# A two-layer encoder on one core: the second block's modulation is made in two pieces, x is loaded in three

## The chip, the cores and the metric

The kernel runs on one core of a Trainium2 chip. The metric is the device time of one execution in microseconds (us), the median of several runs. The engines of the core have short names: PE (TensorE, matrix products), DVE (VectorE), ACT (ScalarE), POOL (GpSimd), and SP (SyncE, which here issues the loads). Each engine works through a fixed list of instructions in order and waits on semaphores where an instruction needs another engine's result or a load.

## The reference

Two layers, a gated linear attention (GLA) and an S5 state-space layer, on one sequence of T = 256 frames with D = 2048 channels, all in float32. A vector c shifts and scales each layer's input. What is cut stands at the first part of layer 0, where the change lies:

```python
mod = jnp.einsum('bd,lde->lbe', jax.nn.silu(c), ada_w) + ada_b[:, None, :]
for i in range(DEPTH):
    shift, scale, gate = jnp.split(mod[i], 3, axis=-1)
    u = x * (1.0 + scale[:, None, :]) + shift[:, None, :]
...
    # GLA: u @ w_in, then
    q, k, v, z, g_lr = jnp.split(
        proj, [GLA_QK, 2 * GLA_QK, 2 * GLA_QK + D_INNER, 2 * GLA_QK + 2 * D_INNER], axis=-1)
```

So before v, q and k can be computed from any 128 channels of u, the shift and the scale of these channels are needed: each is a product of silu(c) (2048 long) with 128 columns of `ada_w`.

## The kernel before

**Tiles and blocks.** The 2048 channels are 16 k-tiles of 128 partitions. The projections v (4096 columns, 8 groups of 512) and q and k (2048 columns, 4 groups of 512, called q here) need all 16 k-tiles. The kernel runs through them in four blocks of k-tiles, `blocks` = (0,2), (2,4), (6,4), (10,6) (first k-tile, count), so that it can begin with the first two tiles of u while the modulation of the others is still being made. In a block, `vqk_steps` lists the steps: for each of the 8 groups of v, and then the 4 of q, one step for each pair of k-tiles (kp). A step loads 256 x 512 weights (`wload`, 0.5 MB), splits them into a high part (ACT, L145) and a low part (DVE, L146), and issues on PE 12 matmuls of 512 columns for v (`mv_step`, L167 to L169) or 24 of 256 for q (`st_step`, L180 to L182): high weights by high u, low weights by high u, high weights by low u. At the end of a block v's banks are copied to the buffer `vbig` by ACT (first block) or added to it by DVE (L357 before, L372 after the change); q's likewise (L371).

**u.** `u_make(k0, nk)` makes u for k-tiles in twos: PE transposes x (L334, tiles psx), DVE multiplies by the scale and adds the shift (L338, uf), ACT rounds to the high part (L321, u0h), DVE subtracts for the low part (L322, u0l). It runs at the start of each block, for that block's tiles.

**Modulation.** `ada_pe(l, part, k0, nk)` returns a list of operations that make nk k-tiles of the shift (part 0) or of the scale (part 1): nk loads of 1 MB from `ada_w` (tiles named a), each followed by 16/nk products, and at the end `mod_cols`. Without `dve` the products are PE matmuls into a bank psa (L265), copied to a row by ACT (L268). With `dve=True` DVE makes the row: a multiplication by one column of silu(c) (L257) and then a chain of 15 multiply-and-adds (L259), each of nk x 128 columns and each on the result of the last. `mod_cols` turns the row into columns by PE matmuls with one column (L236, psmod), and DVE adds the bias into `mods` (L239 for the shift, L241 for the scale).

**Order.** The main loop (L714 on) spreads the modulation operations for the next block, list `a` made from `pieces[n + 1]`, evenly among the steps of this block. In block 0 it also loads the last 1792 columns of x (after step 0), in block 1 small vectors. The loop's order goes to a scheduler that fixes each engine's list. All loads are issued by SP, in order; eight semaphores go round among them, so a load also waits for the landing of the eighth before. The weights' tiles "w" form a ring of 4 (with 2 more in this part), and a load into it waits until both the high and the low part of the tile last held there are done. x (tiles xrow), modulation tiles and u lie in other slots ("s8").

**Names.** In the lists, v020 is the bank for v group 0 of the block that begins with k-tile 2, frames 0; wv02, hiv02 and lov02 are the weights of v group 0 for kp 2 (k-tiles 4 and 5) and their high and low parts; row012, psa002 and psmod012 are of layer 0, part 1 or 0, k-tile 2 on. a0120 is the load number 0 for row012. Numbers behind an underscore tell tiles of one name apart.

Of the kernel before, what the change touches and what calls it, by code (L numbers as in the profile page):

```python
# [16 lines left out]
D = 2048  # L17
# [16 lines left out]
def trunk(ctx, tc, x, c, ln_g, ln_b, ada_w, ada_b, gla_w_in, gla_gate_w2, gla_gate_b, gla_norm_g,  # L34
# [3 lines left out]
    V, S, PE = nc.vector, nc.scalar, nc.tensor  # L38
# [187 lines left out]
    cz = tp.tile([P, 16, 32], F32, tag="cz", name="cz")  # L226
# [5 lines left out]
    def mod_cols(row, l, part, k0, nk):  # L232

        ps = psx(f"psmod{l}{part}{k0}")
        for i in range(nk):
            PE.matmul(ps[:, i:i + 1], lhsT=row[:, i * P:(i + 1) * P], rhs=ones[:, 0:1], start=True, stop=True)  # L236
        ab = abT[:, 32 * l + 16 * part + k0:32 * l + 16 * part + k0 + nk]
        if part == 0:
            V.tensor_tensor(mods[:, l, 0, k0:k0 + nk], ps[:, 0:nk], ab, op=ALU.add)  # L239
        else:  # L240
            V.scalar_tensor_tensor(mods[:, l, 1, k0:k0 + nk], ps[:, 0:nk], 1.0, ab, op0=ALU.add, op1=ALU.add)  # L241

    def ada_pe(l, part, k0, nk, dve=False):

        acc = [None]
        nr, wd = 16 // nk, nk * P

        def step(kq):
            w = s8t(f"a{l}{part}{k0}{kq}", [nr, wd])
            dma(w, ada_w[l, kq * nr * P:(kq + 1) * nr * P, part * D + k0 * P:part * D + k0 * P + wd].rearrange("(k p) c -> p k c", p=P))  # L250
            if dve:
                if kq == 0:
                    acc[0] = rp.tile([P, 512], F32, tag="row", name=f"row{l}{part}{k0}", bufs=2)
                for i in range(nr):
                    k, o = kq * nr + i, acc[0][:, :wd]
                    if k == 0:
                        V.tensor_scalar(o, w[:, i, :], cs[:, 0:1], None, op0=ALU.mult)  # L257
                    else:
                        V.scalar_tensor_tensor(o, w[:, i, :], cs[:, k:k + 1], o, op0=ALU.mult, op1=ALU.add)  # L259
                return  # L260
            if kq == 0:
                acc[0] = psx(f"psa{l}{part}{k0}")
            for i in range(nr):
                k, q = kq * nr + i, i % 4
                PE.matmul(acc[0][32 * q:32 * q + 32, :wd], lhsT=cz[:, k, :], rhs=w[:, i, :], start=(k < 4), stop=(k >= 12))  # L265
            if kq == nk - 1:
                row = rp.tile([P, 512], F32, tag="row", name=f"row{l}{part}{k0}", bufs=2)
                S.copy(row[:, :wd], acc[0][:, :wd])  # L268
                acc[0] = row

        return [lambda kq=kq: step(kq) for kq in range(nk)] + [lambda: mod_cols(acc[0], l, part, k0, nk)]

    gate_dst = [None, None]

# [37 lines left out]
    def x_load(c0, c1):  # L312
        if not xr:
            xr.extend([s8t(f"xrow{i}", [D]) for i in range(2)])
        for tt in range(2):
            dma(xr[tt][:, c0:c1], x[0, tt * P:(tt + 1) * P, c0:c1])
# [11 lines left out]
    def u_make(k0, nk):  # L328
        for k2 in range(k0, k0 + nk, 2):
            ps = psx(f"psx{k2}")  # L330
            for kk in range(2):
                for tt in range(2):
                    k = k2 + kk
                    PE.transpose(ps[:, kk * T + tt * P:kk * T + (tt + 1) * P], xr[tt][:, k * P:(k + 1) * P], ident)  # L334
            for kk in range(2):
                k = k2 + kk
                uf = tp.tile([P, T], F32, tag="uf", name=f"uf{k}", bufs=2)
                V.tensor_scalar(uf, ps[:, kk * T:(kk + 1) * T], mods[:, 0, 1, k:k + 1], mods[:, 0, 0, k:k + 1], op0=ALU.mult, op1=ALU.add)  # L338
                hilo(u0.hi(k), u0.lo(k), uf)
# [63 lines left out]
    S.copy(abT, ps[:, :64])  # L403

    blocks = ((0, 2), (2, 4), (6, 4), (10, 6))
    pieces = (((0, 2),), ((2, 4),), ((6, 4),), ((10, 4), (14, 2)))
    ada0[-1]()
    x_load(0, 256)
    early = more(2, 0)
# [302 lines left out]
        gl["ft"] = ft  # L712

    gate = gla_gate()  # L714
    for n, blk in enumerate(blocks):
        u_make(*blk)
        steps = vqk_steps(*blk)
        a = []
        if n + 1 < len(blocks):
            for pc in pieces[n + 1]:  # L720
                a += ada_pe(0, 0, *pc) + ada_pe(0, 1, *pc, dve=pc[0] < 10)
        done = 0
        for i, f_ in enumerate(steps):
            while done < len(a) * (i + 1) // len(steps):
                a[done]()
                done += 1
            f_()
            if n == 0 and i == 0:
                x_load(256, D)
            if n == 1 and i == 0:  # L730
                vectors()
            if n == 2:
                next(lam, None)
                if i == 8:
                    prep_small()
            elif n == 3:
                pump(V_RATE)
                if i >= GATE_AT:
                    next(gate, None)
        if n == 2:  # L740
            for _ in lam:
                pass
# [6 lines left out]
    for c0, w_, o in ((0, 4, 0), (1, 3, 4), (2, 2, 7)):  # L749
        a = s8t(f"qs{c0}", [8, w_, 64])  # L750
# [10 lines left out]
    for h in range(4):  # L761
        ps = psx(f"psst{h}")
        for cc, (r, a, b) in enumerate(((0, 0, 256), (64, 64, 256), (0, 256, 384), (64, 320, 384))):
            for t in range(2):
                PE.matmul(ps[r:r + 64, a:b], lhsT=kt[:, 2 * h + t, cc * 64:cc * 64 + 64], rhs=qs[cc][:, 2 * h + t, :],
                          start=(t == 0), stop=(t == 1))
# [593 lines left out]
```

## Time and profile before

| | us |
|---|---|
| three runs | 1855.99, 1858.26, 1859.24 |
| median | 1858.26 |
| profiled execution, whole | 1856.07 |
| its span | 1854.3 |
| mean granted clock of PE | 0.994 |

The span is the time from the first to the last instruction in the profiled execution; what lies around it is 1.8 us. The profiled execution is 2.2 us below the median. In the profile, a row of a timeline gives start, duration (summed where several like instructions follow each other, "x8"), engine, source line, operation, output and inputs, and in brackets the idle time before it with what ended it. The granted clock is 1.0 at full speed and 0.5 at half.

### The profile page before, as it was taken

What the parts mean: (1) busy time and instruction counts of PE and PEld (TensorE: products, weight loads), DVE (VectorE), ACT (ScalarE), POOL (GpSimd) and SP (SyncE); (2) the same over time, 40 slices, a digit from 0 to 9 for tenths busy, and PEclk for the clock granted to TensorE, in tenths of its full rate; (3) what the DMA queues carried; (4) which work ended last, traced back from release to release, by engine and by line L of the source; (5) the groups of instructions that cost most, each with busy time, mean ns of one, the idle gap of its engine ahead of it and who ended that gap; (6) DMA issues with size and microseconds to landing.
All of it is one profiled execution on the core that took longest, in us unless ns stands there. A gap on an engine that the chain in (4) does not pass through costs nothing.

```text
span 1854.3 us, 33845 instructions
## 1 busy us (share of the span) xinstructions
PE 1802.9 (97%) x13635; PEld 1587.3 (86%) x13635; DVE 1423.6 (77%) x1886; ACT 894.9 (48%) x1247; POOL 68.8 (4%) x76
## 2 busy tenths in 40 slices
PE   6999999999999999999999999999999999999997
PEld 3787798799999888799998999989888888888886
DVE  2788675989999988688799789888677775557556
ACT  3533365655556333654444444545544444444332
POOL 0000000000000000002222210000000000000000
PEclk9999999999999999999999999999999999999999
DMA  9887976789889998565555477899788886669653
GB/s 357 316 270 259 350 240 209 213 298 322 285 285 318 332 356 285 173 204 163 157 165 158 136 210 216 237 241 247 222 271 267 270 274 211 186 186 328 193 189 91
DMA packets 239494, 449.15 MB, mean 242 GB/s; under 512 B 19221, under 2 KB 45263, under 8 KB 238055
## 3 DMA queue, kind: packets, MB, share of 16 engines
q1 hardware_dynamic: 235400, 437.53, 73.5%
q0 software_dynamic: 3168, 8.41, 1.5%
q8 instruction: 107, 1.75, 0.4%
q10 hardware_dynamic: 768, 1.05, 0.2%
q14 instruction: 51, 0.41, 0.1%
HBM read 432.49 MB, written 14.42 MB: 241 GB/s over the span
## 4 chain that ended last, share of the span: by engine, by line
PE 70%; DVE 8%; DMA 4%; issue 2%; ACT 1%; SPq 0%; DVEq 0%; ACTq 0%
PE gl L192 13%; PE gl L193 6%; PE op L168 6%; PE op L169 6%; PE op L167 6%; PE z L182 3%; PE z L180 3%; PE z L181 3%; PE sz L180 3%; PE sz L182 2%; PE sz L181 2%; PE su L180 2%; PE su L181 2%; PE su L182 2%; DMA rb<-rec 1%
## 5 line engine op out<-in xcount | busy, mean ns | idle before, releaser
L146 DVE TENSOR_TENSOR logl<-wgl,higl 128x1024 fp32r<-128x1024 f32 x128 | 156.5, 1224 | 117.1 <-ACT higl L145 110.2
L145 ACT CAST higl<-wgl 128x1024 fp32r<-128x1024 f32 x128 | 134.3, 1050 | 174.6 <-PE gl L192 169.7
L192 PE MATMUL gl<-yp,higl 128*128 128x512 f32 x512 | 180.7, 398 | 0.1
L192 PE MATMUL gl<-yb,higl 128*128 128x512 f32 x512 | 178.7, 394 | 0.0
L145 ACT CAST hio<-wo 128x1024 fp32r<-128x1024 f32 x96 | 101.2, 1055 | 156.2 <-PE op L169 138.2
L146 DVE TENSOR_TENSOR loo<-wo,hio 128x1024 fp32r<-128x1024 f32 x96 | 117.3, 1223 | 67.0 <-ACT hio L145 66.4
L292 DVE SCALAR_TENSOR_TENSOR acc<-wa,cs,acc 128x512 f32<-128x512 f32 x215 | 160.8, 748 | 2.7
L180 PE MATMUL su<-u1h,hisu 128*128 128x256 f32 x512 | 151.8, 298 | 0.0
L180 PE MATMUL sz<-u1h,hisz 128*128 128x256 f32 x512 | 150.1, 293 | 1.2 <-ACT zs L1193 1.2
L180 PE MATMUL z<-u0h,hiz 128*128 128x256 f32 x512 | 148.7, 290 | 0.0
L181 PE MATMUL su<-u1l,hisu 128*128 128x256 f32 x512 | 146.0, 285 | 0.0
L182 PE MATMUL z<-u0h,loz 128*128 128x256 f32 x512 | 145.0, 283 | 0.9 <-DVE loz L146 0.9
L182 PE MATMUL sz<-u1h,losz 128*128 128x256 f32 x512 | 145.2, 284 | 0.4 <-DVE losz L146 0.4
L182 PE MATMUL su<-u1h,losu 128*128 128x256 f32 x512 | 145.5, 284 | 0.0
L181 PE MATMUL sz<-u1l,hisz 128*128 128x256 f32 x512 | 145.2, 284 | 0.0
L181 PE MATMUL z<-u0l,hiz 128*128 128x256 f32 x512 | 144.7, 283 | 0.0
L193 PE MATMUL gl<-yb,logl 128*128 128x256 f32 x512 | 142.7, 279 | 0.0
L193 PE MATMUL gl<-yp,logl 128*128 128x256 f32 x512 | 141.4, 279 | 0.0
L192 PEld LDWEIGHTS gl<-yp,higl 128*128 128x128 f32 x512 | 95.9, 188 | 23.7 <-issue 1.7
L145 ACT CAST hisz<-wsz 128x1024 fp32r<-128x1024 f32 x64 | 66.9, 1050 | 100.9 <-PE sz L181 66.2
L192 PEld LDWEIGHTS gl<-yb,higl 128*128 128x128 f32 x512 | 96.0, 187 | 22.4
L145 ACT CAST hisu<-wsu 128x1024 fp32r<-128x1024 f32 x64 | 66.8, 1049 | 92.8 <-PE su L181 79.7
(316 smaller groups left out, 5021.9 us busy)
## 6 DMA issues: line engine op xcount, KB each, us to landing
wgl<-in_s_w_glu SPq DMA_DIRECT2D x128, 512.0 KB, 4.6
wa<-in_ada_w SPq DMA_DIRECT2D x115, 512.0 KB, 4.9
a<-in_ada_w SPq DMA_DIRECT2D x32, 1024.0 KB, 10.9
wv<-in_gla_w_in SPq DMA_DIRECT2D x64, 512.0 KB, 6.1
wz<-in_gla_w_in SPq DMA_DIRECT2D x64, 512.0 KB, 5.2
wsu<-in_s_w_in SPq DMA_DIRECT2D x64, 512.0 KB, 3.8
wsz<-in_s_w_in SPq DMA_DIRECT2D x64, 512.0 KB, 4.1
wo<-in_s_w_out SPq DMA_DIRECT2D x64, 512.0 KB, 4.5
```

The costliest lines, as they stand in the source:

```text
L145: S.copy(hi, w)
L146: last_lo[0] = V.tensor_tensor(lo, w, hi.bitcast(F32), op=ALU.subtract).ins
L167: PE.matmul(banks[tt], lhsT=uh, rhs=hi[:, kk, :], start=(k == first), stop=False)
L168: PE.matmul(banks[tt], lhsT=uh, rhs=lo[:, kk, :], start=False, stop=False)
L169: PE.matmul(banks[tt], lhsT=ul, rhs=hi[:, kk, :], start=False, stop=(k == last))
L180: PE.matmul(o, lhsT=wh, rhs=u.hi(k), start=(k == first), stop=False)
L181: PE.matmul(o, lhsT=wh, rhs=u.lo(k), start=False, stop=False)
L182: PE.matmul(o, lhsT=wl, rhs=u.hi(k), start=False, stop=(k == last))
L192: PE.matmul(banks[f], lhsT=hi[:, kk, fs], rhs=u.both(k), start=(k == 0), stop=False)
L193: PE.matmul(banks[f][:, :T], lhsT=lo[:, kk, fs], rhs=u.hi(k), start=False, stop=(k == last))
L292: V.scalar_tensor_tensor(acc[0], w[:, kk, :], cs[:, k:k + 1], acc[0], op0=ALU.mult, op1=ALU.add)
```

## The change

The modulation of the second block, k-tiles 2 to 5, is made in two pieces of two k-tiles each instead of one of four. The scale of the first piece (DVE) comes first, then its shift (PE), then u for k-tiles 2 and 3; the same then for k-tiles 4 and 5. The last three operations for the second piece (the last PE products of the shift with the row's copy, its columns, and u for k-tiles 4 and 5) are kept back from block 0 and run in block 1, after its first two steps. These first steps are reordered, so that groups 0 and 1 of v use k-tiles 2 and 3 before either uses 4 and 5. For the later blocks, u is made in the block before, when the modulation is done. The PE products of these pieces are issued in twos (`pair`): two loads, then the products of both. x is loaded in columns 0 to 255, 256 to 767 (after step 1 of block 0) and 768 to 2047 (in block 1) instead of 0 to 255 and 256 to 2047. In the third piece of the list DVE still makes the scale, now ahead of the shift; for the last two pieces PE makes both, the scale in twos.

```diff
@@ -240,9 +240,10 @@
         else:
             V.scalar_tensor_tensor(mods[:, l, 1, k0:k0 + nk], ps[:, 0:nk], 1.0, ab, op0=ALU.add, op1=ALU.add)
 
-    def ada_pe(l, part, k0, nk, dve=False):
-
-        acc = [None]
+    def ada_pe(l, part, k0, nk, dve=False, pair=False):
+
+
+        acc, ws = [None], []
         nr, wd = 16 // nk, nk * P
 
         def step(kq):
@@ -258,17 +259,31 @@
                     else:
                         V.scalar_tensor_tensor(o, w[:, i, :], cs[:, k:k + 1], o, op0=ALU.mult, op1=ALU.add)
                 return
-            if kq == 0:
+            ws.append(w)
+            if not pair:
+                mults(kq)
+
+        def mults(kq):
+            if acc[0] is None:
                 acc[0] = psx(f"psa{l}{part}{k0}")
-            for i in range(nr):
-                k, q = kq * nr + i, i % 4
-                PE.matmul(acc[0][32 * q:32 * q + 32, :wd], lhsT=cz[:, k, :], rhs=w[:, i, :], start=(k < 4), stop=(k >= 12))
+            k = nr * (kq + 1 - len(ws))
+            while ws:
+                w = ws.pop(0)
+                for i in range(nr):
+                    q = k % 4
+                    PE.matmul(acc[0][32 * q:32 * q + 32, :wd], lhsT=cz[:, k, :], rhs=w[:, i, :], start=(k < 4), stop=(k >= 12))
+                    k += 1
             if kq == nk - 1:
                 row = rp.tile([P, 512], F32, tag="row", name=f"row{l}{part}{k0}", bufs=2)
                 S.copy(row[:, :wd], acc[0][:, :wd])
                 acc[0] = row
 
-        return [lambda kq=kq: step(kq) for kq in range(nk)] + [lambda: mod_cols(acc[0], l, part, k0, nk)]
+        ops = []
+        for kq in range(nk):
+            ops.append(lambda kq=kq: step(kq))
+            if pair and kq % 2:
+                ops.append(lambda kq=kq: mults(kq))
+        return ops + [lambda: mod_cols(acc[0], l, part, k0, nk)]
 
     gate_dst = [None, None]
 
@@ -403,7 +418,7 @@
     S.copy(abT, ps[:, :64])
 
     blocks = ((0, 2), (2, 4), (6, 4), (10, 6))
-    pieces = (((0, 2),), ((2, 4),), ((6, 4),), ((10, 4), (14, 2)))
+    pieces = (((0, 2),), ((2, 2), (4, 2)), ((6, 4),), ((10, 4), (14, 2)))
     ada0[-1]()
     x_load(0, 256)
     early = more(2, 0)
@@ -712,21 +727,32 @@
         gl["ft"] = ft
 
     gate = gla_gate()
+    u_make(*blocks[0])
     for n, blk in enumerate(blocks):
-        u_make(*blk)
         steps = vqk_steps(*blk)
         a = []
         if n + 1 < len(blocks):
             for pc in pieces[n + 1]:
-                a += ada_pe(0, 0, *pc) + ada_pe(0, 1, *pc, dve=pc[0] < 10)
+                dve = pc[0] < 10
+                a += ada_pe(0, int(dve), *pc, dve=dve) + ada_pe(0, int(not dve), *pc, pair=True)
+                a.append(lambda pc=pc: u_make(*pc))
+        over = []
+        if n == 0:
+
+            a, over = a[:-3], a[-3:]
+        elif n == 1:
+            steps[0:4] = [steps[0], steps[2], steps[1], steps[3]]
+            steps[1:2] = [lambda f_=steps[1]: (f_(), [g_() for g_ in late])]
         done = 0
         for i, f_ in enumerate(steps):
             while done < len(a) * (i + 1) // len(steps):
                 a[done]()
                 done += 1
             f_()
-            if n == 0 and i == 0:
-                x_load(256, D)
+            if n == 0 and i == 1:
+                x_load(256, 768)
+            if n == 1 and i == 3:
+                x_load(768, D)
             if n == 1 and i == 0:
                 vectors()
             if n == 2:
@@ -737,6 +763,7 @@
                 pump(V_RATE)
                 if i >= GATE_AT:
                     next(gate, None)
+        late = over
         if n == 2:
             for _ in lam:
                 pass
```

Products of a piece of two k-tiles have 256 columns instead of 512, and a load (1 MB in each case) carries 8 of them instead of 4.

The order of the engines' instructions moves at three places. The first is DVE's list in block 0, from the low half of the second v group on. Before:

```order
L146 TENSOR_TENSOR lov10_236<-wv10_233,hiv10_235 128x1024
L146 TENSOR_TENSOR lov20_264<-wv20_261,hiv20_263 128x1024
L146 TENSOR_TENSOR lov30_292<-wv30_289,hiv30_291 128x1024
L146 TENSOR_TENSOR lov40_322<-wv40_319,hiv40_321 128x1024
L239 TENSOR_TENSOR mods_108<-psmod002_339,abT_143 128x4
L146 TENSOR_TENSOR lov50_350<-wv50_347,hiv50_349 128x1024
L146 TENSOR_TENSOR lov60_372<-wv60_369,hiv60_371 128x1024
L257 TENSOR_SCALAR row012_391<-a0120_389,cs_101 128x512
```

With the change, the same place:

```order
L146 TENSOR_TENSOR lov10_248<-wv10_245,hiv10_247 128x1024
L146 TENSOR_TENSOR lov20_276<-wv20_273,hiv20_275 128x1024
L258 TENSOR_SCALAR row012_202<-a0120_200,cs_101 128x256
L260 SCALAR_TENSOR_TENSOR row012_202<-a0120_200,cs_101,row012_202 128x256 x7
L260 SCALAR_TENSOR_TENSOR row012_202<-a0121_233,cs_101,row012_202 128x256 x8
L241 SCALAR_TENSOR_TENSOR mods_108<-psmod012_267,abT_143 128x2
L146 TENSOR_TENSOR lov30_300<-wv30_297,hiv30_299 128x1024
L146 TENSOR_TENSOR lov40_324<-wv40_321,hiv40_323 128x1024
```

The whole row of the first piece's scale, sixteen operations, now stands between the low halves of v groups 2 and 3, with the addition that waits for PE's columns behind it; before, the row (of 512 columns) began after group 6. The second place is PE's list from the end of block 0 into block 1. Before:

```order
L182 MATMUL q303_559<-u0h0_109,loq30_563 128x256
L236 MATMUL psmod012_550<-ones0_84,row012_391 128x1 x4
L334 MATMUL psx2_594<-ident_89,xrow0_151 128x128
L334 MATMUL psx2_594<-ident_89,xrow1_152 128x128
L334 MATMUL psx2_594<-ident_89,xrow0_151 128x128
L334 MATMUL psx2_594<-ident_89,xrow1_152 128x128
L334 MATMUL psx4_607<-ident_89,xrow0_151 128x128
L334 MATMUL psx4_607<-ident_89,xrow1_152 128x128
L334 MATMUL psx4_607<-ident_89,xrow0_151 128x128
L334 MATMUL psx4_607<-ident_89,xrow1_152 128x128
L390 MATMUL psv_646<-ident_89,vr_640 128x104
```

With the change, block 0's last q matmul is followed at once by block 1's first steps (k-tiles 2 and 3), and the second piece's shift, columns and transposes stand behind these, ahead of the second pass of v group 0:

```order
L167 MATMUL v121_661<-hiv11_664,u0h0_109 128x512
L168 MATMUL v121_661<-lov11_665,u0h0_109 128x512
L169 MATMUL v121_661<-hiv11_664,u0l0_111 128x512
L274 MATMUL psa004_680<-a0040_582,cz_105 32x256 x8
L274 MATMUL psa004_680<-a0041_584,cz_105 32x256 x8
L236 MATMUL psmod004_699<-ones0_84,row004_697 128x1 x2
L349 MATMUL psx4_703<-ident_89,xrow0_151 128x128
L349 MATMUL psx4_703<-ident_89,xrow1_152 128x128
L349 MATMUL psx4_703<-ident_89,xrow0_151 128x128
L349 MATMUL psx4_703<-ident_89,xrow1_152 128x128
L167 MATMUL v020_624<-hiv02_718,u0h0_109 128x512
L167 MATMUL v021_625<-hiv02_718,u0h0_109 128x512
```

What stood at the boundary, four columns and eight transposes for four k-tiles, is now half in block 0 and half behind block 1's first two steps. The third place is DVE's list at block 1's beginning. Before, from the scale's addition on:

```order
L241 SCALAR_TENSOR_TENSOR mods_108<-psmod012_550,abT_143 128x4
L338 TENSOR_SCALAR uf2_599<-psx2_594,mods_108 128x256
L338 TENSOR_SCALAR uf3_603<-psx2_594,mods_108 128x256
L146 TENSOR_TENSOR lov02_652<-wv02_649,hiv02_651 128x1024
L322 TENSOR_TENSOR u0l0_111<-uf2_599,u0h0_109 128x256
L322 TENSOR_TENSOR u0l0_111<-uf3_603,u0h0_109 128x256
L338 TENSOR_SCALAR uf4_612<-psx4_607,mods_108 128x256
L338 TENSOR_SCALAR uf5_616<-psx4_607,mods_108 128x256
```

With the change, from the addition of the second piece's scale on:

```order
L241 SCALAR_TENSOR_TENSOR mods_108<-psmod014_540,abT_143 128x2
L258 TENSOR_SCALAR row016_655<-a0160_653,cs_101 128x512
L260 SCALAR_TENSOR_TENSOR row016_655<-a0160_653,cs_101,row016_655 128x512
L239 TENSOR_TENSOR mods_108<-psmod004_699,abT_143 128x2
L260 SCALAR_TENSOR_TENSOR row016_655<-a0160_653,cs_101,row016_655 128x512
L353 TENSOR_SCALAR uf4_708<-psx4_703,mods_108 128x256
L260 SCALAR_TENSOR_TENSOR row016_655<-a0160_653,cs_101,row016_655 128x512
L337 TENSOR_TENSOR u0l0_111<-uf4_708,u0h0_109 128x256
L353 TENSOR_SCALAR uf5_712<-psx4_703,mods_108 128x256
L146 TENSOR_TENSOR lov02_719<-wv02_716,hiv02_718 128x1024
L337 TENSOR_TENSOR u0l0_111<-uf5_712,u0h0_109 128x256
L260 SCALAR_TENSOR_TENSOR row016_655<-a0161_736,cs_101,row016_655 128x512 x2
```

The products of block 2's scale (row016) now begin here, among the second piece's u; thirteen of the row's sixteen operations stand between the shift's addition (L239) and the low half of v group 3 for kp 2 (lov32). Before, row016 began after the low half of v group 6.

## The prediction

> **What bounds the kernel now.** First the page: busy time, the 40 slices, the chain that ended last.
>
> ```profile
> span 1854.3 us, 33845 instructions
> PE 1802.9 (97%) x13635; PEld 1587.3 (86%) x13635; DVE 1423.6 (77%) x1886; ACT 894.9 (48%) x1247; POOL 68.8 (4%) x76
> PE   6999999999999999999999999999999999999997
> PE 70%; DVE 8%; DMA 4%; issue 2%; ACT 1%; SPq 0%; DVEq 0%; ACTq 0%
> ```
>
> PE is busy 97% of the span, so TensorE is the bound nearly everywhere, and an edit that leaves the number of matmuls alone can only win or lose the moments in which PE waits or runs at half clock. The change touches the order of work up to about 260 us; behind that every engine has the same instructions in the same order. So the time moves by as much as that place moves. Next, who PE waits for from 20 to 262 us (line, releaser, total, times, longest).
>
> ```profile
> PE v L168 <- DVE lov L146: 3.3, 5, 1.0
> PE psmod L236 <- DVE row L259: 2.8, 1, 2.8
> PE v L167 <- ACT u0h L321: 2.1, 2, 1.1
> PE v L167 <- ACT hiv L145: 1.9, 3, 0.6
> PE psa L265 <- DMA a<-in_ada_w: 1.1, 1, 1.1
> ```
>
> Some 11 us in all can be won here by perfect cover. The largest single wait, 2.8 us, is the one the change takes away: PE at block 1's start, waiting for the scale's products. The timeline of PE at that place (start, duration, form, idle before):
>
> ```profile
> 68.66 0.28 PE L182 MATMUL q<-u0h,loq 128*128 128x256 f32 x1
> 71.72 1.84 PE L236 MATMUL psmod<-ones,row 128*128 128x1 f32 x8 [2.79 <-DVE row L259]
> 73.42 1.95 PE L334 MATMUL psx<-ident,xrow 128*128 128x128 f32 x8
> 75.17 0.38 PE L390 MATMUL psv<-ident,vr 104*128 104x104 f32 x1
> 75.59 0.79 PE L167 MATMUL v<-hiv,u0h 128*128 128x512 f32 x1
> ```
>
> From the last q matmul of block 0 (ending 68.9) to block 1's first v matmul (75.59) pass 6.7 us. Now windows as long as the clock's steps (start:end, length, busy PE PEld DVE ACT POOL, granted clock, DMA share, GB/s):
>
> ```profile
> 67.46:70.87 3.41, 1.47 (x13) 1.27 (x11) 3.23 (x6) 2.08 (x4) 0.00 (x0) 1.00 1.04 384
> 70.87:74.28 3.41, 2.56 (x12) 2.59 (x13) 0.87 (x2) 0.00 (x0) 0.00 (x0) 0.50 1.05 387
> 74.28:77.70 3.42, 3.37 (x12) 2.59 (x11) 3.14 (x6) 0.95 (x3) 0.00 (x0) 0.50 0.53 195
> 77.70:81.11 3.41, 3.41 (x16) 2.81 (x16) 2.78 (x6) 2.82 (x4) 0.00 (x0) 1.00 0.55 159
> ```
>
> A window in which PE was busy 1.47 of 3.41 us is followed by two at half clock. A wait of some 2 us can therefore cost another 1.5 or so. The Trainium skill ("TensorE: Matmul & The Clock Gate", What's actually happening) states that the gate closes after an idle window of about 3.4 us; here it closed after one that was 43% busy, so the trace is stricter. By the page's word the broken waits that I forecast below would leave the clock full, about 1.5 us less.
>
> **What goes.** The 6.7 us at block 1's start: u for k-tiles 2 and 3 is made in block 0, so v 0 of block 1 follows the last q directly. Further on, u of blocks 2 and 3 is made in the block before, which ends these waits:
>
> ```profile
> 152.08 0.50 PE L167 MATMUL v<-hiv,u0h 128*128 128x512 f32 x1 [1.05 <-ACT u0h L321]
> 162.97 0.64 PE L265 MATMUL psa<-a,cz 128*32 128x512 f32 x4 [1.09 <-DMA a<-in_ada_w]
> 196.52 0.50 PE L168 MATMUL v<-lov,u0h 128*128 128x512 f32 x1 [0.99 <-DVE lov L146]
> 207.61 0.50 PE L168 MATMUL v<-lov,u0h 128*128 128x512 f32 x1 [0.83 <-DVE lov L146]
> ```
>
> The first (1.05) goes, with about 0.2 at block 3. The products by twos may end the 1.09. The last two are DVE's, and DVE gets more in block 2, not less: I take −1.3 for these, with 0 and −4 as ends.
>
> **What comes in block 0.** Rows that price its steps: of DVE by form from 20 to 262 us (count | busy us, mean ns | idle before), of ACT likewise, and of the timelines of DVE, ACT and PE.
>
> ```profile
> L146 DVE TENSOR_TENSOR lov<-wv,hiv 128x1024 fp32r<-128x1024 f32 x40 | 48.3, 1220 | 23.3 <-ACT hiv L145 23.2
> L259 DVE SCALAR_TENSOR_TENSOR row<-a,cs,row 128x512 f32<-128x512 f32 x30 | 22.5, 748 | 0.6
> L357 DVE TENSOR_TENSOR vbig<-vbig,v 128x512 f32<-128x512 f32 x32 | 21.6, 684 | 19.0 <-PE v L169 18.9
> L371 DVE SCALAR_TENSOR_TENSOR qk<-q,qk 128x256 f32<-128x256 f32 x36 | 14.2, 421 | 8.3 <-PE q L182 8.2
> L338 DVE TENSOR_SCALAR uf<-psx,mods 128x256 f32<-128x256 f32 x16 | 8.0, 538 | 1.7 <-PE psx L334 1.6
> L322 DVE TENSOR_TENSOR u0l<-uf,u0h 128x256 fp32r<-128x256 f32 x16 | 6.6, 421 | 2.1 <-ACT u0h L321 2.0
> 65.32 6.26 DVE L259 SCALAR_TENSOR_TENSOR row<-a,cs,row 128x512 f32<-128x512 f32 x8
> 26.07 0.58 ACT L359 COPY vbig<-v 128x512 f32<-128x512 f32 x1 [3.73 <-PE v L169]
> 27.39 0.64 PE L265 MATMUL psa<-a,cz 128*32 128x512 f32 x4
> 99.27 0.50 PE L167 MATMUL v<-hiv,u0h 128*128 128x512 f32 x1
> 99.61 0.39 PE L168 MATMUL v<-lov,u0h 128*128 128x512 f32 x1
> 99.84 0.39 PE L169 MATMUL v<-hiv,u0l 128*128 128x512 f32 x1
> 56.87 0.39 PE L180 MATMUL q<-u0h,hiq 128*128 128x256 f32 x1 [0.24 <-ACT hiq L145]
> 98.29 1.05 PE L265 MATMUL psa<-a,cz 128*32 128x512 f32 x6
> L145 ACT CAST hiv<-wv 128x1024 fp32r<-128x1024 f32 x20 | 20.9, 1050 | 19.5 <-PE v L169 19.3 <-PE q L181 0.2
> 102.33 0.69 DVE L357 TENSOR_TENSOR vbig<-vbig,v 128x512 f32<-128x512 f32 x1 [0.68 <-PE v L169]
> ```
>
> The row at 65.32 holds eight products, each waiting for the one before: 6.26/8 = 0.78 us a piece. The trace has no product of 256 columns with a column of scalars. Its cost lies between the pace of the independent ones of L371 (0.42 each, starts some 0.35 apart) and 0.78; 0.78 less the (748 − 421 =) 0.33 between the two widths is 0.45; I take 0.52, with 0.07 more for a chain whose hand-over need not shrink with the width. Sixteen products of 512 become 32 of 256, by my price 32 × 0.52 − 16 × 0.78 = 4.2 us more for DVE.
>
> Against this part of the change speaks a rule of the Trainium skill ("VectorE: DVE Perf Modes", The TRN2 errata): an operation that reads SBUF pays a fixed latency per instruction, so small tiles pay it often. By the page's (N + 151)/0.96 ns a product would take 0.42 us for 256 columns and 0.69 for 512, an estimate of 32 × 0.42 − 16 × 0.69 = 2.4 us more for DVE instead of 4.2, and a wait in block 0 shorter by 1.6 us. The rows lie somewhat above it for 512 (748 ns) and on it for 256 (421).
>
> In the new order on DVE, sixteen of these stand behind the low half of v 2 and ahead of that of v 3. Their start: v 0's first copy at 26.07, two cold matmuls of v 1 now ahead of it (some 0.8 from 99.61's 0.23 pitch doubled), copy 0.5, cast 1.05, low half 1.14: 29.0 to 29.5. They end near 29 + 16 × 0.52 = 37.3. PE has done v 0 by 27.4 (without that psa), and v 1 and v 2 (12 matmuls each at 99.84 − 99.61 = 0.23, 2.75 a step) by 32.9; then it stands at psmod012 for the row. **The wait is 4.4 us**, and half clock behind it, +1.5. Ends: with 0.35 a product 1.7 us and no half clock; with 0.78, 8.6.
>
> From 37.3 PE has five v steps (13.8), 16 products of the shift of 256 columns instead of 512 (row 98.29: six take 1.05 + pipelining, four 1.0 us; so 2.0 instead of 4.0), transposes and columns 0.7, 96 q matmuls (56.87 to 68.9, 12.0), 1.5 for the clock and about 1.5 for the short waits for hi and lo that stay: 37.3 + 13.8 + 2.0 + 0.7 + 12.0 + 3.0 = 68.8. Block 0 ends where it ended before: the new wait eats what the shorter shift frees. The x load in three pieces costs nothing here: it puts 1.3 MB behind the weights, and the DMA, at 385 GB/s throughout, delivers each weight earlier.
>
> **What comes in block 1.** PE runs v 0 and v 1 with k-tiles 2 and 3 (2 × 2.75 and 0.5 of columns) to 74.8, then 16 products of the shift of the second piece, 2.0, to 76.8. Now comes a serial chain that before lay in the 6.7 us: ACT's row copy 0.5, columns on PE 0.4 and an addition 0.2 (78.1 by then, with hand-overs), uf of k-tile 4, its high part, uf and low part of 5 (0.5 + 0.4 + 0.5 + 0.4), among them in DVE's order two products for block 2's scale (1.5) and lov of v 0 (1.2): v 0 goes on at 82.2. PE has 1.4 us of work in these 5.4, so it **idles 4.0 us**. Without DVE's further queue, v 0 to v 3 would end 2.3 + 5 × 2.75 = 16.0 later, at 98.2.
>
> But DVE's queue is what ends last. From the addition at 78.1 to the low half of v 3's second pass its order holds 13 products of 512 (13 × 0.78 = 10.1), 6 low halves (6 × 1.22 = 7.3), 6 additions to vbig (6 × 0.68 = 4.1), 2 uf and 2 u low (1.9): 23.4, less some 0.07 for each of 29 pieces that starts before the last has ended: 21.5. So that half is not there before 99.7, and v 3 ends 2.3 later, **at 102.0**. With the waits that the order forces (walked row by row: 2.9 for PE at v 1's first additions, 2.1 at v 2's, of which half is made good) 104.0 warm; with the half clock that the 4 us bring, 105.6. Before, these products came later in block 1, from v 5 on, each between halves that had time. The like point of before is the end of v 3 at 102.1 (99.27 + 12 × 0.23; DVE adds its last bank at 102.33), with three groups of block 2's shift already done, 3.0 us that the new order does later: 99.1.
>
> **The sum.** The point behind block 1's v 3 moves by +2.9 (DVE's sum alone), +4.9 (with the waits) or +6.5 (with the clock as well). I take +5.8, between the last two: the clock's windows run on by themselves, and the 4 us of idling are broken by 1.4 of work. Blocks 2 and 3 give −1.3. Together **+4.5 us**. The profiled run took 1856.07 us (1854.3 and 1.8 around it), 2.2 under the median of 1858.26; a shift doesn't depend on that, so 1858.26 + 4.5 = **1862.8 us**. The bounds are 2.9 − 4.0 = −1.1 and +6.5; a product at 0.35 or at 0.78 moves them by −4.3 and +4.2 more (block 0's wait), to −5.4 and +10.7.
>
> **Rivals.**
>
> (a) *Cheap products.* If a 256-column product costs DVE 0.35 instead of 0.52, the wait in block 0 is 1.7 instead of 4.4, the clock stays (1.5), and everything up to the chain comes 4.3 us earlier. The bunch in block 1 ends at 102.1 − 4.3 = 97.8, −1.3 against 99.1; blocks 2 and 3 then give up to −4, their waits for DVE and DMA gone too. −5, **1853**. For it: L371's pace. Against it: 0.78 for the chained row of 512, above its duration of 0.75. The two ends, +4.5 at 0.52 and −5 at 0.35, cross zero at some 0.44 us a product. Chance 0.22.
>
> (b) *An exchange.* One wait for another: DVE's sum alone holds in block 1 (+2.9), the clock falls once and not twice, blocks 2 and 3 give −1.3 to −2. **1859.5**. For it: DVE stands idle 23.3 us before its low halves in the stretch, so a bunch can be made good; against it: the in-order queue. Chance 0.35.
>
> (c) *DVE holds block 2 too.* There the products of 512 of the next scales stand close to low halves whose waits already show 0.99 and 0.83; a bunch there, one stalled step of 1.2 and one of 2.2 by the same walk, adds 3.4 us, **1866.2**. Chance 0.13, within "slower".
>
> **How the numbers follow.** My forecast +4.5 gets 0.30, (c) 0.13, (b) 0.35, (a) 0.22. A measurement here tells about 0.2%, 3.7 us, from no change: faster than 1854.5 is (a); between, (b) and little of the forecast; slower than 1862.0, the rest. That makes 0.22, 0.35, 0.43. The range leaves out a tenth on either side: below, (a)'s end with the four small waits gone, 1851; above, (c) with a half clock more, 1869.
>
> **What would show it.** In the trace of the changed kernel: no wait at block 1's start; a wait of PE at psmod of two columns near 33 us, 4.4 long, and half clock behind it (0 to 2 us: (a)); block 0's last q near 68.8; a broken wait of about 4 us from 77 on with clock 0.50; v 3's second pass waiting for lov; v 2 of block 2 without the 1.05. The duration of the row with 256 columns decides between forecast and (a). What makes it wrong: the order of DMAs bringing a weight later than reckoned, in block 1 above all, where the scale's and the shift's weights stand ahead of v 0's second half.

## The result: 13 us slower, outside the range

| | median us (lowest to highest, runs) | ratio to before, 95% interval |
|---|---|---|
| before | 1858.75 (1855.99 to 1864.68, 4) | |
| changed | 1873.32 (1871.66 to 1873.76, 4) | 1.0067 [1.0051, 1.0083] |
| changed, once more (e5) | 1871.84 (1869.85 to 1876.04, 5), beside before at 1859.78 (29 runs) | 1.0069 [1.0055, 1.0083] |

The forecast was 1862.8 with 1851 to 1869 as its range: the sign was that of the likeliest case, the size was three times as large. The page of the changed kernel (busy time, slices, chain that ended last):

```profile
span 1871.1 us, 33944 instructions
PE 1807.4 (97%) x13667; PEld 1592.3 (85%) x13667; DVE 1427.2 (76%) x1904; ACT 897.3 (48%) x1248; POOL 69.2 (4%) x76
PE   6899999999999999999999999999999999999997
PE 80%; DVE 10%; DMA 5%; issue 2%; ACT 2%; SPq 1%; DVEq 0%; ACTq 0%
```

PE is busy for the same share of the span as before, 97%. What PE waits for from 20 to 290 us, where the program was changed (line, releaser, total, times, longest):

```profile
PE v L168 <- DVE lov L146: 9.6, 6, 2.3
PE psmod L236 <- DVE row L260: 4.9, 1, 4.9
PE v L167 <- ACT u0h L336: 2.4, 2, 1.3
PE pspw L578 <- ACT lc L580: 1.1, 2, 0.6
PE pspw L578 <- ACT pd L571: 1.0, 1, 1.0
PE psmod L236 <- ACT row L278: 0.5, 1, 0.5
```

The wait for the row moved from block 1's start to block 0 and grew from 2.8 to 4.9 us. Waits for low halves, 3.3 before (to 262 us), are 9.6. The new waits, one by one, in PE's timeline (start, duration, form, idle before):

```profile
37.26 0.98 PE L236 MATMUL psmod<-ones,row 128*128 128x1 f32 x4 [4.88 <-DVE row L260]
...
78.97 0.60 PE L236 MATMUL psmod<-ones,row 128*128 128x1 f32 x4 [0.49 <-ACT row L278]
79.44 0.63 PE L349 MATMUL psx<-ident,xrow 128*128 128x128 f32 x4
81.38 0.73 PE L167 MATMUL v<-hiv,u0h 128*128 128x512 f32 x2 [1.31 <-ACT u0h L336]
83.53 0.50 PE L168 MATMUL v<-lov,u0h 128*128 128x512 f32 x1 [1.41 <-DVE lov L146]
90.18 0.50 PE L168 MATMUL v<-lov,u0h 128*128 128x512 f32 x1 [2.03 <-DVE lov L146]
99.04 0.50 PE L168 MATMUL v<-lov,u0h 128*128 128x512 f32 x1 [1.52 <-DVE lov L146]
188.45 0.50 PE L168 MATMUL v<-lov,u0h 128*128 128x512 f32 x1 [2.05 <-DVE lov L146]
201.39 0.50 PE L168 MATMUL v<-lov,u0h 128*128 128x512 f32 x1 [2.34 <-DVE lov L146]
```

From 77 to 100 us there are five waits of 6.8 us together, then two of 4.4 in block 2. The clock, in windows of 3.41 us laid so that the granted clock changes only at their ends (start:end, length, busy time of PE, PEld, DVE, ACT, POOL, granted clock, DMA share, GB/s):

```profile
33.02:36.44 3.42, 0.00 (x0) 0.00 (x0) 3.21 (x7) 1.05 (x1) 0.00 (x0) 1.00 1.08 369
36.44:39.85 3.41, 2.59 (x10) 1.62 (x10) 1.95 (x4) 0.00 (x0) 0.00 (x0) 0.50 1.04 385
39.85:43.26 3.41, 3.41 (x13) 1.76 (x12) 0.00 (x0) 0.00 (x0) 0.00 (x0) 0.50 1.09 356
...
80.81:84.22 3.41, 1.43 (x5) 0.91 (x6) 3.41 (x7) 2.25 (x4) 0.00 (x0) 1.00 1.05 388
84.22:87.64 3.42, 3.42 (x10) 2.63 (x9) 2.36 (x5) 0.46 (x1) 0.00 (x0) 0.50 1.02 378
87.64:91.05 3.41, 1.38 (x6) 0.81 (x6) 2.48 (x3) 1.05 (x1) 0.00 (x0) 1.00 0.20 75
91.05:94.46 3.41, 3.41 (x10) 2.67 (x9) 2.15 (x3) 0.32 (x1) 0.00 (x0) 0.50 0.55 154
```

In block 1 two windows are at half clock, where I had counted on one; in block 0 there are two as well, behind the wait for the row.

**Where the time came from.** Both kernels have a second profile (e5, e6 below), so that the spread of one and the same program is seen. Starts of the same matmuls in PE's timelines, in us:

| start of | before | before, e6 | changed | changed, e5 | shift of the means | forecast |
|---|---|---|---|---|---|---|
| block 0's last q | 68.66 | 69.26 | 69.90 | 68.72 | +0.35 | 0 |
| block 2's first v | 152.08 | 152.93 | 160.30 | 159.41 | +7.35 | +4.75 |
| first z matmul | 375.60 | 378.05 | 385.85 | 386.70 | +9.45 | +4.5 |
| last psy of the S5 layer | 1302.49 | 1310.42 | 1318.94 | 1317.60 | +11.8 | +4.5 |
| last PE instruction | 1847.25 | 1854.54 | 1864.37 | 1863.40 | +13.0 | +4.5 |

The rows for the first z matmul, in the order of the table (one from each kernel's timeline):

```profile
375.60 0.36 PE L180 MATMUL z<-u0h,hiz 128*128 128x256 f32 x1
```

```profile
378.05 0.36 PE L180 MATMUL z<-u0h,hiz 128*128 128x256 f32 x1
```

```profile
385.85 0.36 PE L180 MATMUL z<-u0h,hiz 128*128 128x256 f32 x1
```

```profile
386.70 0.36 PE L180 MATMUL z<-u0h,hiz 128*128 128x256 f32 x1
```

The reader is to see that two executions of one program (the kernel before) stand 2.45 us apart here, and 7.3 at the end. What stands out of that spread is +7.35 up to block 2 and +9.45 up to z.

### The profile page after: what moved, and what is told of

Same layout as the page of the kernel before. It is cut to its first block, busy times and chain, and to the rows that moved or that the text cites. A ratio compares the mean times of both kernels' runs of the same rounds, so it can differ in the third digit from the quotient of the medians.

```text
span 1871.1 us, 33944 instructions
## 1 busy us (share of the span) xinstructions
PE 1807.4 (97%) x13667; PEld 1592.3 (85%) x13667; DVE 1427.2 (76%) x1904; ACT 897.3 (48%) x1248; POOL 69.2 (4%) x76
## 3 DMA queue, kind: packets, MB, share of 16 engines
q10 hardware_dynamic: 768, 1.05, 0.2%
## 4 chain that ended last, share of the span: by engine, by line
PE 80%; DVE 10%; DMA 5%; issue 2%; ACT 2%; SPq 1%; DVEq 0%; ACTq 0%
PE gl L192 13%; PE gl L193 6%; PE op L168 6%; PE op L167 6%; PE op L169 6%; PE z L182 3%; PE z L180 3%; PE z L181 3%; PE sz L180 3%; PE v L168 3%; PE v L167 3%; PE v L169 3%; PE sz L182 2%; PE sz L181 2%; DMA rb<-rec 2%
## 5 line engine op out<-in xcount | busy, mean ns | idle before, releaser
L192 PEld LDWEIGHTS gl<-yp,higl 128*128 128x128 f32 x512 | 95.8, 187 | 23.5 <-issue 1.5
L168 PE MATMUL v<-lov,u0h 128*128 128x512 f32 x256 | 104.8, 409 | 10.6 <-DVE lov L146 10.6
```

The source lines that it names most:

```text
L168: PE.matmul(banks[tt], lhsT=uh, rhs=lo[:, kk, :], start=False, stop=False)
L192: PE.matmul(banks[f], lhsT=hi[:, kk, fs], rhs=u.both(k), start=(k == 0), stop=False)
```

## The experiments

**e1: the third block's scale back behind its shift.** What the change did in one line to block 2's modulation is undone:

```diff
-                a += ada_pe(0, int(dve), *pc, dve=dve) + ada_pe(0, int(not dve), *pc, pair=True)
+                if pc[0] == 6:
+                    a += ada_pe(0, 0, *pc) + ada_pe(0, 1, *pc, dve=True)
+                else:
+                    a += ada_pe(0, int(dve), *pc, dve=dve) + ada_pe(0, int(not dve), *pc, pair=True)
```

> The change, but the modulation of the third block (k-tiles 6 to 9) in the old order: its shift on PE first, its scale on DVE behind, so that the products row016 leave the beginning of block 1. Theory 1 (the products bunched in DVE's queue hold block 1): the low halves of v groups 1 to 3 of block 1 are no longer late (waits 2.0, 1.5 and 0.3 us in the changed kernel), the clock stays full after 90 us, and block 2's first v matmul starts 4 to 5 us earlier than in the changed kernel, at about 156 instead of 160.3; time some 4.5 us below the changed kernel's 1873.3. Rival (the kept-back chain at 77 to 84 us and its half clock hold block 1, and the products only fill DVE's idle time): block 2 starts less than 1.5 us earlier, time within 2 us of the changed kernel.

Measured: 1862.72 us (10 runs; 1.0020 [1.0005, 1.0034] to before), some 10 below the changed kernel. Block 2's first v matmul in PE's timeline, and PE's waits from 60 to 160 us:

```profile
151.99 0.40 PE L167 MATMUL v<-hiv,u0h 128*128 128x512 f32 x1
```

```profile
PE v L168 <- DVE lov L146: 1.0, 3, 0.5
PE v L167 <- ACT hiv L145: 1.0, 1, 1.0
PE psmod L236 <- ACT row L278: 0.5, 1, 0.5
PE psa L274 <- DMA a<-in_ada_w: 0.4, 1, 0.4
```

Theory 1 holds, and more strongly than I had put it: block 2 starts 7.9 us earlier than the changed kernel's 159.9 (mean), not 4 to 5. The waits for low halves in that stretch fall from 5.3 to 1.0. Of the two windows at half clock the second is gone (the granted clock from 90 to 97 us is 1.00), the first, behind the kept-back chain, stays (0.77 from 83 to 90). The edit also undoes the issue by twos of this piece's shift on PE; no run separates that from the order, but the waits that go are those for DVE's low halves.

**e2: the first piece's scale behind its shift.**

```diff
-                a += ada_pe(0, int(dve), *pc, dve=dve) + ada_pe(0, int(not dve), *pc, pair=True)
+                if pc[0] == 2:
+                    a += ada_pe(0, 0, *pc, pair=True) + ada_pe(0, 1, *pc, dve=True)
+                else:
+                    a += ada_pe(0, int(dve), *pc, dve=dve) + ada_pe(0, int(not dve), *pc, pair=True)
```

> The change, but the first piece (k-tiles 2 and 3) with its shift on PE first and its scale on DVE behind. Theory 1 (the wait of 4.9 us for row012 at 32 us and the half clock behind it are a loss of block 0): block 0's last q matmul starts at 65 to 66.5 instead of 69.9, and the time falls by 3 to 4 us against the changed kernel. Rival (block 0 is paced by its loads, the wait only stands where another would): the last q stays within 1.5 us of 69.9, and waits for hi and lo take the place of the one for the row.

Measured: 1868.25 us (4 runs, 1865.27 to 1873.56; 1.0060 [1.0039, 1.0081]). Block 0's last q starts at 68.54. PE's waits from 20 to 70 us:

```profile
PE v L167 <- ACT hiv L145: 2.0, 2, 1.6
PE v L168 <- DVE lov L146: 1.6, 3, 0.5
PE v L167 <- ACT u0h L336: 1.1, 1, 1.1
PE psmod L236 <- ACT row L278: 0.6, 1, 0.6
PE psmod L236 <- DVE row L260: 0.2, 1, 0.2
```

The largest wait of the changed kernel, 4.9 us, is gone, and block 0 ends as it does in e5's profile of the changed kernel (68.72). For block 0 the rival is right: other waits stand in its place. A wait of 4.9 us cost block 0 nothing that can be told. That the loads pace block 0, the rival's reason, is not shown by this.

The time fell by 3.6 to 5.1 us against the changed kernel's medians, as theory 1 had it, but its interval holds the changed kernel's ratio, and what the trace gains is not in block 0. PE's list in block 1 moved too, which the edit did not aim at: 12 of v's matmuls, not 24, stand ahead of the kept-back chain, whose products begin at 72.48 us instead of 76.54. No window of block 1 is at half clock (granted clock 1.00 from 68.66 to 154.88), and block 2 begins 5 us earlier than in the changed kernel:

```profile
154.88 0.40 PE L167 MATMUL v<-hiv,u0h 128*128 128x512 f32 x1
```

**e3: only u of blocks 2 and 3 made early,** in the kernel before:

```diff
+    u_make(*blocks[0])
     for n, blk in enumerate(blocks):
-        u_make(*blk)
+        if n == 1:
+            u_make(*blk)
...
                 a += ada_pe(0, 0, *pc) + ada_pe(0, 1, *pc, dve=pc[0] < 10)
+                if n:
+                    a.append(lambda pc=pc: u_make(*pc))
```

> The kernel before, with one thing of the change: u of blocks 2 and 3 is made in the block before (block 1's u stays at its start). Theory 1: the wait of 1.05 us and the work around it at block 2's start go; block 2's first v matmul follows block 1's last q within 0.3 us instead of 2.2, of which some 1.0 is work moved; from there on -1.3 us, time 1857.5 against 1858.75 before. Rival: the adding of u's work to DVE's queue in block 1 costs as much, 0.

Measured: 1858.97 beside 1858.99 (1.0004 [0.9992, 1.0015]). Block 2 starts at 151.16, 1.35 before the mean of the kernel before, and the first z matmul at 376.69 is level with its mean of 376.8. The rival: what the start of block 2 gains is lost inside it, to waits for DVE's low halves (2.0 us at 196.6, none of that length before).

**e9: as e1, and nothing is kept back** for block 1; the chain of k-tiles 4 and 5 runs in block 0's q steps:

```diff
         if n == 0:
-            a, over = a[:-3], a[-3:]
-        elif n == 1:
-            steps[0:4] = [steps[0], steps[2], steps[1], steps[3]]
-            steps[1:2] = [lambda f_=steps[1]: (f_(), [g_() for g_ in late])]
+            pass
```

> As e1 (the change with the third block's scale behind its shift), and nothing is kept back from block 0: shift, columns and u for k-tiles 4 and 5 run in block 0's q steps, block 1's steps are in the old order. Theory 1 (the chain in block 1 costs its idling, 2.0 us in e1, and one window at half clock, 1.6): block 1's v runs without a wait, block 2's first v matmul starts at 148 to 149 us instead of e1's 152.0, and the time is 3 to 4 us below e1's 1862.7. Rival (the same chain stalls block 0's q steps, whose load of the shift's second half stands behind the q weights): a wait of 3 us or more before 70 us, block 2's start within 1 us of e1.

Measured: 1858.64 (12 runs; 0.9995 [0.9981, 1.0009]). Theory 1 has the time, and each theory has a part of the places: block 2 starts at 150.29, 1.7 earlier than e1 instead of 3 to 4, and block 0 ends later (last q at 74.75), with waits of 0.48 and 1.40 us before 57. From z on it is 3.7 us earlier than e1.

**e12: nothing kept back, the scale ahead of the shift,** the second factor without the first (e9's edit on the changed kernel).

> The change with nothing kept back from block 0 (as e9), but with the third block's scale ahead of its shift as the change has it, so that the products row016 stay at block 1's beginning: the second of the two factors without the first. Theory 1 (the bunch of products holds block 1 by DVE's sum, with or without the chain): waits for low halves in block 1 of 3 us or more, block 2's first v matmul at 154 to 157 us against e9's 150.3, time 4 to 6 us above e9's 1858.6. Rival (the bunch is late only because the kept-back chain lets it start late; without that, DVE has the time): block 2's start within 2 us of e9, time within 2 us of e9, and only both together make the changed kernel's 1872.

Measured: 1867.73 (6 runs; 1.0048 [1.0032, 1.0064]), 9 above e9. Block 2's first v and PE's waits from 60 to 160 us:

```profile
154.92 0.40 PE L167 MATMUL v<-hiv,u0h 128*128 128x512 f32 x1
```

```profile
PE v L168 <- DVE lov L146: 4.2, 5, 1.5
```

Theory 1: the products hold block 1 without the chain too, by 4.6 us at block 2's start. The four kernels together:

| | block 2's first v | first z | time |
|---|---|---|---|
| neither (e9) | 150.29 | 374.94 | 1858.6 |
| chain kept back (e1) | 151.99 | 378.68 | 1862.7 |
| products bunched (e12) | 154.92 | 381.12 | 1867.7 |
| both (changed; means) | 159.85 | 386.3 | 1872 to 1873 |

Alone they cost 1.7 and 4.6 at block 2's start; both cost 9.6, as the chain makes the bunch begin later: in DVE's timelines the bunch goes on at 79.69 and 78.52 us in the two profiles of the changed kernel, at 74.78 in e12. In e2, which has both but an earlier chain, it goes on at 75.63, and block 2 begins at 154.88, as in e12. So the 3.3 us beyond the sum seem to hang on where the chain stands (e2 is one profile); they come with the two windows at half clock, which neither e2 nor e12 has in block 1. In the time they are 4 and 9 alone, and some 14 together.

**e5, e6, e7: how much of it is scatter.** The changed kernel and the kernel before once more, and the kernel before with one more small tile taken from the pool s8, which moves later tiles to other addresses:

```diff
+    spare = s8t("spare", [8])
+    V.memset(spare, 0.0)
     ada0 = ada_pe(0, 0, 0, 2)
```

> The changed kernel itself once more, for its time over more runs and a second profile. In the first profile its S5 stage (first su matmul to last psy matmul) took 534.1 us against 527.9 before, though both programs have the same instructions in the same order there. Theory A (that stage differs from run to run, and the first profile drew a long one): the second profile's stage lies anywhere from 528 to 534, the first part (z's first matmul at 385.9) repeats within 0.3 us, and the median falls to some 1870 (10.3 above before). Theory B (it belongs to this program): 533 to 535 again, median 1872 to 1874.

> The kernel before once more with a second profile. Theory A: the S5 stage anywhere from 528 to 534 us, z's first matmul at 375.6 within 0.3. Theory B: 527 to 529 again. Time 1859 either way.

> The kernel before with one more small tile taken at the start from the pool s8 and zeroed (one DVE instruction of 8 columns): every engine's list stays, but later tiles of that pool lie at other addresses, as they do in the changed kernel. Theory A: time 1859 within 2 us, first part the same. Theory B, if the addresses are what differs: the time moves by 3 us or more with the first part (z's first matmul at 375.6) unmoved.

Measured: e6 took 1861.33 (11 runs; 1.0006 [0.9997, 1.0014]), e7 1861.34 (11 runs; 1.0009 [0.9999, 1.0019]). From its first su to its last psy matmul the S5 layer took 527.9 and 533.4 us in the two profiles of the kernel before, 534.1 and 532.0 in those of the changed, and 528.2 in e7: theory A, and more scatter than it allowed: the first z moved by 0.85 (changed) and 2.45 us (before) between executions, not by 0.3, and stands at 379.19 in e7. PE's longest waits in that layer, in the two profiles of the one program:

```profile
PE pswb L1010 <- ACT wbt L1011: 3.7, 4, 1.3
PE psy L1166 <- DMA mt<-dk: 3.1, 3, 2.0
```

```profile
PE pswb L1010 <- ACT wbt L1011: 5.6, 4, 3.1
PE psy L1166 <- DMA mt<-dk: 3.4, 4, 2.0
```

So the first profile of the kernel before, on which the forecast stood, was one of its short ones, and some of the 6 us that the first pair of profiles shows in S5 is no work of the change.

**e4, e8, e10, e11: is there a better order?** e4 takes the kernel before, makes u of every later block in the block before, and calls block 1's modulation one step sooner in the q steps; e11 is e4 once more, e8 is e4 with u of blocks 2 and 3 at their own start, e10 the same to e9.

```diff
-            while done < len(a) * (i + 1) // len(steps):
+            while done < min(len(a), len(a) * (i + 1) // len(steps) + (n == 0 and i >= 7)):
```

> The kernel before, modulation of block 1 in one piece of four k-tiles, shift first, as before; but its operations are called one step sooner in the q steps of block 0, so that the last two loads of the scale stand ahead of the first two q weights, and u of every later block is made in the block before. Theory 1 (the 6.7 us at block 1's start come only from where the last products and u stand in the order, and no splitting is needed): block 1's first v matmul starts at 69 to 71 instead of 75.6, no half clock there, block 2 starts without its wait: 6 to 8 us below the kernel before, about 1852. Rival (the wait for the row moves into q's first steps, through the low half that stands behind the products in DVE's order): a wait of 3 us or more near 57 us, time within 2 us of before.

> The kernel with the modulation called one step sooner (e4), but u of blocks 2 and 3 made at their own start again, as before; only block 1's u is made early. If making u early for blocks 2 and 3 costs DVE's queue more than it saves (e3: first z matmul 1.1 us later), this is 1 to 2 us faster than e4 by the first part, z's first matmul at about 374.5 instead of 375.8, time about 1853.5. If not, block 2's wait of 1.05 comes back and it is 1 us slower than e4.

> As e9, with u of blocks 2 and 3 made at their own start, as before. By e3 making them early costs the first part 0.5 to 1.1 us, by e4 against e8 it gains 1.7: theory 1 (DVE's queue in block 2, as in e3): 1 us below e9; rival: 1 to 2 us above e9.

> e4 once more. If its 4 us under the kernel before are its own: median 1853 to 1857 again and ratio below 0.999. If they came of the scatter that the later stages show from run to run: 1858 to 1860, as the first part of its profile (z's first matmul at 375.8, before 375.6 and 378.1) would have it.

Measured: e4 1854.82 (10 runs; 0.9981 [0.9972, 0.9990]), e11, the same kernel, 1857.43 (12 runs; 0.9994 [0.9982, 1.0007]); e8 1860.37 (12 runs; 1.0000 [0.9988, 1.0013]); e10 1860.93 (12 runs; 1.0008 [0.9995, 1.0021]). The stall of e4 shows where its rival had put it (PE's waits from 20 to 80 us; the two longest end at 55.55 and 58.68, though neither reaches the rival's 3 us):

```profile
PE v L168 <- DVE lov L146: 3.8, 4, 2.4
PE v L167 <- ACT hiv L145: 3.5, 4, 1.6
```

Block 1 begins at 77.05 in e4, later than the 75.59 of before: the last products stand ahead of a low half that block 0 needs. What it has won by block 2 (151.38 against a mean of 152.5) is about 1 us. Two sets of runs of one kernel gave −4.2 and −0.9 us, and the interval of the second holds 1, so I don't call it a better version; no other kernel here beats the one before. Early u of blocks 2 and 3 seems worth more in these orders than in e3: without it the first z comes at 377.49 (e8) after 375.80 and 375.20 (e4, e11), and at 378.46 (e10) after 374.94 (e9). The gains that theory 1 of e8 and of e10 forecast did not come. That leaving early u out costs anything is likely only for e10 (3.5): the 1.7 to 2.3 us of e8 are less than the 2.45 between two executions of one program.

## Why the prediction was wrong

By the table of starts 8.5 us are missing from the forecast: 2.6 arose up to block 2 (the term +5.8 for block 1), 2.35 in blocks 2 and 3 (the term −1.3), and 3.5 behind the first z matmul, where I had put nothing.

**Right.** The price of a product of 256 columns: 15 of them took 7.78 us, 0.52 each, as taken, and rival (a) fell with it. From DVE's timeline of the changed kernel, and its sums by form from 20 to 110 us:

```profile
28.95 0.35 DVE L258 TENSOR_SCALAR row<-a,cs 128x256 f32<-128x256 f32 x1
29.34 7.78 DVE L260 SCALAR_TENSOR_TENSOR row<-a,cs,row 128x256 f32<-128x256 f32 x15
...
L260 DVE SCALAR_TENSOR_TENSOR row<-a,cs,row 128x256 f32<-128x256 f32 x30 | 14.5, 484 | 0.9
```

The Trainium skill's price ("VectorE: DVE Perf Modes", The TRN2 errata: 0.42 us, an estimate by its formula) is given there for an fp32 `tensor_tensor` addition and lies below what this operation takes, 0.484 us as the mean of 30 and 0.52 from start to start in its chain; the trace decides.

The wait in block 0 was forecast at 4.4 and was 4.9 and 4.2 in two profiles. That block 0 ends where it did, and that PE goes straight into block 1, held: the last q starts at 69.90 and 68.72, where the forecast had block 0 end at 68.8, and the first v of block 1 at 70.02, right behind the 69.90. The half clock behind that wait, booked at 1.5 us, was two windows in the first profile and one in the second. Of the chain I had idling of 4.0; the three waits of 0.49, 1.31 and 1.41 are 3.2.

**Wrong in size: block 1.** The mechanism, 13 products in DVE's order ahead of the low half of v 3, is the one that cost the time (e1, e12). DVE's timeline shows the bunch:

```profile
86.11 0.75 DVE L260 SCALAR_TENSOR_TENSOR row<-a,cs,row 128x512 f32<-128x512 f32 x1
87.64 0.69 DVE L372 TENSOR_TENSOR vbig<-vbig,v 128x512 f32<-128x512 f32 x1 [0.78 <-PE v L169]
88.24 0.74 DVE L260 SCALAR_TENSOR_TENSOR row<-a,cs,row 128x512 f32<-128x512 f32 x1
88.91 1.22 DVE L146 TENSOR_TENSOR lov<-wv,hiv 128x1024 fp32r<-128x1024 f32 x1
92.00 0.69 DVE L372 TENSOR_TENSOR vbig<-vbig,v 128x512 f32<-128x512 f32 x1 [1.88 <-PE v L169]
...
94.74 3.11 DVE L260 SCALAR_TENSOR_TENSOR row<-a,cs,row 128x512 f32<-128x512 f32 x4
97.77 2.35 DVE L146 TENSOR_TENSOR lov<-wv,hiv 128x1024 fp32r<-128x1024 f32 x2
...
103.84 1.22 DVE L146 TENSOR_TENSOR lov<-wv,hiv 128x1024 fp32r<-128x1024 f32 x1
```

The low half that I had put at 99.7 from DVE's sum, and some 2 us later with the waits in it, came at 105.06 (the last row's 103.84 + 1.22). The addition from which I counted came at 79.61 instead of 78.1; from there DVE took 25.5 us and not 21.5 (with the waits 23.5), and stood for PE in 3.6 of them. PE and DVE take turns here: DVE stands for PE's last matmul before it may add (0.78, 1.88), and PE then stands for the low half behind that addition (2.03 at 90.18). I had that in the walk, but with one window at half clock; there were two, and at half clock each PE step that DVE waits for is longer too (0.43 us from matmul to matmul at 84.41, 0.23 at 83.86). The term +5.8 was some 8.4: at block 2's start 7.35 and not 4.75, with the 1.05 that the end of block 2's wait brought in both.

**Not there: −1.3 for the later blocks.** I said myself that DVE gets more in block 2, and still booked the gain of u made early. The start of block 2 gave it (−1.35 in e3), the blocks took it back: from block 2's first v to z the changed kernel takes 225.55 and 227.29 us, the kernel before 223.52 and 225.12, so +2.1; with the edit alone (e3) it is 225.53, +1.2. The 2.05 and 2.34 that PE waits for low halves there are rival (c), which I gave 0.13 and priced at 3.4; it came on top of the forecast.

**Wrong in kind: a constant shift behind 260 us.** The lists of all engines are the same from about 275 us of the changed kernel on (but for which of the eight semaphores a load carries), so that held, but from it I concluded that the time moves by as much as that place does. Behind the first z matmul the means differ by another 3.5 us, while two profiles of the kernel before differ by 4.8 (1471.65 and 1476.49 from z to the last PE instruction). In all fourteen profiles of this case the stretch is 1468.30 (e10) to 1478.52 us (changed); the changed kernel's two, 1478.52 and 1476.70, lie near the upper end, with 1477.44 in e11, which has none of the split. Whether those 3.5 belong to the change isn't settled: e7 found no effect of other addresses that stands out of the spread, the semaphores were not tested, and no run tells more.

The clock bears on the rule that I weighed. The Trainium skill ("TensorE: Matmul & The Clock Gate", What's actually happening) asks for an idle window before half clock. Here the first half clock does follow such a window (33.02 to 36.44), but in block 1 windows in which PE was busy 1.43 and 1.38 of 3.41 us (from 80.81 and 87.64, shown above) were each followed by one at 0.50. The trace decides against the page's wording: broken waits dropped the clock, as they had at block 1's start before.

## What to carry to other kernels

A wait that is taken from one engine's path is paid for by whatever is now earlier in the other engine's in-order list: list what stands between the old and the new place of moved work on that engine, and ask which of its entries the first engine needs next. Here swapping two parts of a modulation, one line, moved thirteen vector products ahead of low halves that TensorE was about to need and cost 9 of the 13 us (e12 beside e9), while the stall that the change was made around, 6.7 us with its half clock, was replaced by others of about the same sum (e9: 0.9995 of before). And take two profiles of a kernel before trusting one as the base: here one stage of one program differed by 5.5 us.

## What was not expected of the hardware

The first is the cost of turns at half clock: in the changed kernel's block 1 two windows of 3.4 us came at half clock through waits of 1.3 to 2.0 us none of which is as long as a window. The second is the spread: the S5 layer, with the same list of instructions on every engine, took 527.9 and 533.4 us in two executions of the kernel before, and its waits for ACT's copies 3.7 and 5.6.
